# A block sum of the down projection on GpSimd, and the residual rows loaded at other units

## The chip, the cores and the metric

The kernel runs on one core of a Trainium2 chip. The core has a matrix engine (TensorE, in the profile PE, with its weight loads as PEld), a vector engine (VectorE, DVE), a scalar engine (ScalarE, ACT), GpSimd (POOL) and a queue that issues DMAs (SyncE, SP). Each runs its own instructions in order and waits for the others on semaphores. The metric is the device time of one execution in microseconds (us): the median of the runs.

## The reference

One encoder block on a sequence of 2048 positions with a model width of 1024, all in float32. An RMS norm, a projection, two groups of heads and an output projection come first; then

```
x = x + conv_ffn(rms_norm(x))      # up projection, causal convolution, SiLU gate, down projection
out = rms_norm(x)

conv_ffn: (silu(g) * val) @ w_down # (2048 x 2816) times (2816 x 1024)
```

The change lies in the last product, `@ w_down`, and in the sum with the residual `x` behind it.

## The kernel before

The kernel is one long program in stages: projection, attention and gating, output projection, up projection, and last the down projection, `down()`, which starts near 1985 us of the span. The sequence is worked in two halves of 1024 positions. Activations go through DRAM: the gated result of the up projection is in `act_d[half][f]` (22 blocks of 128 channels by 1024 positions), the residual rows of a half in `rows_d[half][i]` (8 tiles of 128 positions by 1024 columns, 512 KB each).

**Products.** For each half the down projection is a 2 x 2 block product made with seven products in place of eight (a scheme of Strassen's kind): positions are split into two blocks of 512, columns into two of 512, channels into two groups of 11 blocks. The products run in the order P1, P2, P7, P6, P5, P4, P3, each over the 11 block pairs j. One (half, product, j) is a **unit**; there are 2 x 7 x 11 = 154, counted from 0, so P2 of half 0 starts at unit 11, P7 at 22, P6 at 33, P5 at 44. A unit is 12 matmuls: four tiles t of 128 positions, each with three matmuls, because float32 is done with a high and a low part of each operand (high x high, high x low, low x high).

**Preparation.** `prep(u)` readies unit u. It loads the weights `wr` (512 columns; 256 KB) from `w_down` or from weight sums made earlier (`tw_d`), splits them with `both()` (ACT casts the high part `wh`, line 1017; DVE subtracts for the low part `wl`, line 1018), loads the activation blocks it needs (`x11`, `x12`, `x21`, `x22`, 256 KB each, kept for the rest of the half), forms the block sum that its product takes, and splits that into `xh` and `xl` in the same way. The sums are: P7 x11 - x21 into `xs` (line 1346); P6 x21 + x22 in place (line 1349) and from it minus x11 (line 1351); P5 takes x21 as it then is, and beside it x12 - x11 in place (line 1355) for P3. All these have both inputs in SBUF. `ready(u)` calls `prep` two units ahead of the matmuls; there are five buffers for each of the split parts, and four for `wr`.

**Banks.** There are eight accumulators in PSUM, in two banks of four (A and B). P1 starts in A and P2 in B; after P2, B is begun anew by P7. P6, P5 and P3 go on accumulating in A, P4 in B. After each product the four tiles are added to the residual rows (line 1479, the eviction: PSUM plus SBUF). The plan says to which rows and columns:

```
PLAN = dict(P1=("A", 0, 0, False), P2=("B", 0, 0, True), P7=("B", 1, 1, False), P6=("A", 1, 0, False),
            P5=("A", 1, 1, True), P4=("B", 1, 0, True), P3=("A", 0, 1, True))
```

The entries are the bank, the block of rows (0: row tiles 0 to 3, 1: row tiles 4 to 7), the column half, and whether that part is then complete. So P1 and P2 both add to rows 0 to 3, and P7 is the first to add to rows 4 to 7. Where the next product goes on in the same bank (P6 to P5), its first matmul waits for the eviction of that tile. P2, P6 and P3 end with a tail in which the last units are done tile by tile, so that evictions can start before the product has ended.

**Rows.** `row(half, i)` loads a row tile at its first call and afterwards returns what is there. It is called in the loop over units (which loads ahead) and in the eviction loop (`x = row(half, 4 * blk + t)`). Rows 0 to 3 and rows 4 to 7 have four buffers each. The load is tied behind the last weight load issued before it (`issue_after(self.w_ins)`).

**Order.** The order within each engine's queue and the semaphores are made by the framework: it goes through the program with a timeline of its own, takes what is ready by that timeline in the order of the program text, and fixes the result. On the chip the order of each queue no longer changes. An instruction later in the text may thus stand earlier in its queue: the subtractions of line 1355 for P5, for example, stand in DVE's queue from 2071 us on, while PE is in P7.

At the start of the down projection the last two blocks of the up projection are still finished on DVE (`up_conv`), their results stored by POOL's DMA queue, and the memory of their tiles is then given to the blocks `x12`, `x21`, `x22`. Beside that, POOL does in this stage only small sums of 128 x 1 for the final norm (lines 1402, 1421, 1422).

Of the kernel before, what the change touches and what calls it, by code (L numbers as in the profile page):

```python
# [12 lines left out]
ALU = mybir.AluOpType  # L13
# [67 lines left out]
class Block:  # L81
# [1221 lines left out]
    def down(self):  # L1303
        nc, tc = self.nc, self.tc
        tt = nc.vector.tensor_tensor
# [10 lines left out]
        def ring(tag, i, n, dt=F32):  # L1316

            return self.til(dp, [P, TB], dt, tag + "+" if i % n < 2 else tag)

        def block(half, j, name):  # L1320

            k = half, j, name
            if k not in raw:
                raw[k] = ring(name, j, NJ) if name == "x11" else self.til(pools[name], [P, TB], F32, name)
                f = j + (NJ if name[2] == "2" else 0)
                b = int(name[1]) - 1
                with tc.issue_after(self.w_ins):
                    self.dma(raw[k], self.act_d[half][f][:, b * TB:(b + 1) * TB])
            return raw[k]

        def prep(u):
            half, n, j = units[u]
            w = ring("wr", u, 4)
            src = dict(P1=w_down[:, j, 0:TB], P2=w_down[:, j + NJ, 0:TB], P3=w_down[:, j + NJ, TB:D],
                       P5=self.tw_d[j][:, 0, 0:TB], P7=self.tw_d[j][:, 0, TB:D], P4=self.tw_d[j][:, 1, 0:TB], P6=self.tw_d[j][:, 1, TB:D])[n]
            self.w_ins = self.dma(w, src).ins
            wp = [ring(tag, u, 5, F32R) for tag in ("wh", "wl")]
            self.both(wp, w)
            x = lambda name: block(half, j, name)
            if n == "P1":  # L1340
                v = x("x11")
            elif n == "P2":
                v = x("x12")
            elif n == "P7":
                v = xs.pop() if xs else self.til(dp, [P, TB], F32, "xs")
                tt(v, x("x11"), x("x21"), op=ALU.subtract)
            elif n == "P6":

                tt(x("x21"), x("x21"), x("x22"), op=ALU.add)
                v = x("x11")  # L1350
                tt(v, x("x21"), v, op=ALU.subtract)
            elif n == "P5":
                v = x("x21")

                tt(x("x12"), x("x12"), x("x11"), op=ALU.subtract)
            elif n == "P4":
                v = x("x22")
            else:
                v = x("x12")
            if u == 1:  # L1360

                late.append(dp.tile([P, D], F32, name="gf"))
                xs.append(self.til(dp, [P, TB], F32, "xs"))
            xp = [ring(tag, u, 5, F32R) for tag in ("xh", "xl")]
            self.both(xp, v)
            parts[u] = wp, xp

        def ready(u):
            while len(parts) <= min(u, len(units) - 1):
                prep(len(parts))  # L1370

        def mms(bank, u, t, fresh, last):
            w, x = parts[u]
            j = units[u][2]
            ts = slice(t * P, (t + 1) * P)
            kw = {} if fresh else {"skip_group_check": True}
            for i, k in ((0, 0), (0, 1), (1, 0)):
                nc.tensor.matmul(bank[t], lhsT=x[i][:, ts], rhs=w[k], start=fresh and j == 0 and i + k == 0,  # L1378
                                 stop=last and i == 1, **kw)

        def row(half, i):
            if (half, i) not in rows:
                x = rows[half, i] = self.til(dp if i < 4 else pools["x12"], [P, D], F32, "xo")
                with tc.issue_after(self.w_ins):
                    self.dma(x, self.rows_d[half][i])
            return rows[half, i]

        def square(half, i, col):
            x = row(half, i)
            if (half, i, "s") not in rows:  # L1390
                rows[half, i, "s"] = self.til(dp, [P, 2], F32, "s2")
            jk = jks.pop() if jks else self.til(dp, [P, TB], BF16, "jk")
            nc.scalar.activation(jk, x[:, col * TB:(col + 1) * TB], AF.Square,
                                 accum_out=rows[half, i, "s"][:, col:col + 1])

        def end_row(half, i):
            x, ss = rows[half, i], rows[half, i, "s"]
            rs = self.til(dp, [P, 1], F32, "rs")
            tt(rs, ss[:, 0:1], ss[:, 1:2], op=ALU.add)
            nc.vector.tensor_scalar(rs, rs, 1.0 / D, EPS, ALU.mult, ALU.add)  # L1400
            r = self.til(dp, [P, 1], F32, "rstd")
            nc.gpsimd.tensor_tensor(r, rs, self.mhalf[:, 0:1], op=ALU.pow)
            t0 = half * HALF + i * P
            for col in range(2):
                cs = slice(col * TB, (col + 1) * TB)
                nc.vector.scalar_tensor_tensor(x[:, cs], x[:, cs], r, gf[:, cs], op0=ALU.mult, op1=ALU.mult)
                self.dma(self.out[0, t0:t0 + P, cs], x[:, cs])

        def half_done(i):

            x = row(1, i)
            s = self.til(dp, [P, 1], F32, "rs")
            nc.vector.tensor_scalar(s, rows[1, i, "s"][:, 0:1], D * EPS, None, ALU.add)
            tt(x[:, 0:TB], x[:, 0:TB], gf[:, 0:TB], op=ALU.mult)
            rows[i] = s

        def last_row(i):

            x, ss, s = rows[1, i], rows[1, i, "s"], rows[i]
            r = self.til(dp, [P, 1], F32, "rstd")  # L1420
            nc.gpsimd.tensor_scalar(r, ss[:, 1:2], s, 1.0 / D, ALU.add, ALU.mult)
            nc.gpsimd.tensor_tensor(r, r, self.mhalf[:, 0:1], op=ALU.pow)
            t0 = HALF + i * P
            a, b = slice(0, TB), slice(TB, D)
            nc.vector.scalar_tensor_tensor(x[:, b], x[:, b], r, gf[:, b], op0=ALU.mult, op1=ALU.mult)
            self.dma(self.out[0, t0:t0 + P, b], x[:, b])
            nc.scalar.activation(x[:, a], x[:, a], AF.Copy, scale=r)
            self.dma(self.out[0, t0:t0 + P, a], x[:, a])
# [8 lines left out]
        def finish_up():  # L1437

            with tc.issue_after(low1):
                self.up_conv(NF - 1)  # L1440
            self.fps.close()
            d2 = es.enter_context(tc.tile_pool(name="downp2", side="right", **kw))
            for n in ("x12", "x21", "x22"):
                pools[n] = d2
            self.dma(gf, self.a["norm_final_g"].unsqueeze(0).broadcast_to([P, D]))
# [7 lines left out]
        for half in range(2):  # L1453
            for n in self.PRODUCTS:
                which, blk, col, whole = PLAN[n]
                fresh = n in ("P1", "P2", "P7")
                if fresh:
                    banks[which] = [self.til(pp, [P, TB], F32, "D") for _ in range(4)]
                bank = banks[which]
                tail = {"P2": 2, "P6": 2, "P3": 4 if half else 2}.get(n, 0)  # L1460
                cs = slice(col * TB, (col + 1) * TB)
                for j in range(NJ - tail):
                    if u == 2:
                        finish_up()
                    ready(u + (4 if (half, n) == (1, "P3") else 2))
                    for t in range(4):
                        mms(bank, u, t, fresh, j == NJ - 1)
                    u += 1
                    if (half, n) == (1, "P3") and j < 4:
                        half_done(j)  # L1470
                    if n in ("P1", "P2") and 4 <= j < 8:
                        row(half, j - 4 + (4 if n == "P2" else 0))
                for t in range(4):
                    if tail:
                        ready(u + tail + max(0, t - 1))
                    for m in range(tail):
                        mms(bank, u + m, t, fresh, m == tail - 1)
                    x = row(half, 4 * blk + t)
                    tt(x[:, cs], bank[t], x[:, cs], op=ALU.add)  # L1479
                    if whole:  # L1480
                        square(half, 4 * blk + t, col)
                        if (half, n) == (1, "P3"):
                            last_row(t)
                        elif n in ("P4", "P3"):
                            end_row(half, 4 * blk + t)
                u += tail
# [77 lines left out]
```

## Time and profile before

| | us |
|---|---|
| median of 3 runs | 2423.89 (2420.24 to 2425.25) |
| the profiled execution | 2419.3 |
| its span, first to last instruction | 2417.5 |

Of the page's parts, the busy times are by engine with the share of the span; the chain is the work that ended last, followed back from the end to what released each step; a group of instructions is line, engine, operation, output and inputs by name, shapes and count, then busy time, mean ns of one, and the idle time before them with what ended it. Three lines of the page and of one window give the setting:

```profile
PEclk9999999999999999999999999999999999999999
L1378 PE MATMUL D<-wh,xh 128*128 128x512 f32 x368 | 140.8, 389 | 1.2 <-DVE xo L1479 1.2
L994 POOL TENSOR_TENSOR tw<-tw 128x512 f32<-128x512 f32 x44 | 67.0, 1522 | 44.9 <-DMA tw<-in_w_down_dram 42.9
```

The first is the granted clock of TensorE in 40 slices of the span, at full speed throughout. The second is a group of the down projection's matmuls; one is shown as 389 ns long, but they are pipelined and start 0.23 us apart. The third is a group on POOL in an earlier stage: sums of weights of the same shape as the block sums above.

### The profile page before, as it was taken

What the parts mean: (1) busy time and instruction counts of PE and PEld (TensorE: products, weight loads), DVE (VectorE), ACT (ScalarE), POOL (GpSimd) and SP (SyncE); (2) the same over time, 40 slices, a digit from 0 to 9 for tenths busy, and PEclk for the clock granted to TensorE, in tenths of its full rate; (3) what the DMA queues carried; (4) which work ended last, traced back from release to release, by engine and by line L of the source; (5) the groups of instructions that cost most, each with busy time, mean ns of one, the idle gap of its engine ahead of it and who ended that gap; (6) DMA issues with size and microseconds to landing.
All of it is one profiled execution on the core that took longest, in us unless ns stands there. A gap on an engine that the chain in (4) does not pass through costs nothing.

```text
span 2417.5 us, 33292 instructions
## 1 busy us (share of the span) xinstructions
PE 2392.8 (99%) x11288; PEld 1998.3 (83%) x11288; DVE 1764.8 (73%) x3108; ACT 1355.3 (56%) x2652; POOL 323.2 (13%) x315
## 2 busy tenths in 40 slices
PE   9999999999999999999999999999999999999998
PEld 7888888988888888888888888888888888888887
DVE  6447776665568778878878774598888877857875
ACT  4246767644456555767677764365555455454444
POOL 4114140100241221211111101100000000000001
PEclk9999999999999999999999999999999999999999
DMA  8673635668855444555445555312222238438633
GB/s 278 182 241 111 206 100 175 186 192 265 260 191 183 160 163 161 165 173 185 146 151 182 170 195 203 116 53 96 79 86 81 87 96 310 157 99 300 205 118 122
DMA packets 246042, 400.58 MB, mean 166 GB/s; under 512 B 51224, under 2 KB 110744, under 8 KB 244448
## 3 DMA queue, kind: packets, MB, share of 16 engines
q1 hardware_dynamic: 240832, 374.34, 47.9%
q0 software_dynamic: 5040, 24.12, 2.5%
q8 instruction: 89, 1.46, 0.2%
q14 instruction: 81, 0.66, 0.1%
HBM read 304.79 MB, written 93.72 MB: 165 GB/s over the span
## 4 chain that ended last, share of the span: by engine, by line
PE 87%; DMA 2%; DVE 1%; ACT 1%; issue 0%; POOL 0%; POOLq 0%; SPq 0%; ACTq 0%; DVEq 0%
PE mm L211 37%; PE D L1378 16%; PE A L1176 3%; PE A L1178 3%; PE A L1177 3%; PE o L822 3%; PE o L821 3%; PE s L773 2%; PE s L772 2%; PE s L834 2%; PE s L833 2%; PE B L1178 2%; PE B L1177 2%; PE B L1176 2%; PE C L1176 1%; PE C L1177 1%
## 5 line engine op out<-in xcount | busy, mean ns | idle before, releaser
L211 PE MATMUL mm<-tlo,whi 128*128 128x512 f32 x896 | 351.4, 392 | 0.0
L211 PE MATMUL mm<-thi,wlo 128*128 128x512 f32 x896 | 351.1, 392 | 0.0
L211 PE MATMUL mm<-thi,whi 128*128 128x512 f32 x896 | 350.5, 391 | 0.5 <-DVE vn L519 0.5
L211 PE MATMUL mm<-whi,thi 128*128 128x512 f32 (+2 forms) x768 | 275.9, 360 | 6.1 <-DVE vn L519 4.4
L211 PE MATMUL mm<-wlo,thi 128*128 128x512 f32 (+2 forms) x768 | 275.5, 359 | 2.2 <-DVE wlo L164 2.2
L211 PE MATMUL mm<-whi,tlo 128*128 128x512 f32 (+2 forms) x768 | 274.8, 358 | 0.0
L150 POOL TENSOR_SCALAR whi<-raw 128x1024 fp32r<-128x1024 f32 (+3 forms) x114 | 132.4, 1163 | 963.2 <-PE mm L211 741.5
L781 ACT ACTIVATE s<-s,part 128x512 f32<-128x512 f32 (+3 forms) x261 | 154.7, 593 | 145.3 <-DVE part L776 80.6
L211 PEld LDWEIGHTS mm<-thi,whi 128*128 128x128 f32 x896 | 168.4, 188 | 35.2 <-issue 0.7
L211 PEld LDWEIGHTS mm<-thi,wlo 128*128 128x128 f32 x896 | 168.5, 188 | 34.1
L211 PEld LDWEIGHTS mm<-tlo,whi 128*128 128x128 f32 x896 | 168.5, 188 | 33.7
L845 DVE TENSOR_TENSOR pl<-e,ph 128x512 fp32r<-128x512 f32 (+1 forms) x218 | 142.9, 662 | 69.6 <-ACT ph L844 40.5
L211 PEld LDWEIGHTS mm<-whi,thi 128*128 128x128 f32 x768 | 145.9, 190 | 26.3 <-DVE vn L519 4.6
L164 DVE TENSOR_TENSOR wlo<-raw,whi 128x1024 fp32r<-128x1024 f32 (+2 forms) x106 | 135.1, 1276 | 44.0 <-POOL whi L150 43.0
L839 ACT ACTIVATE e<-s 128x512 f32<-128x512 f32 (+1 forms) x222 | 114.5, 530 | 91.8 <-DVE s L837 44.0
L211 PEld LDWEIGHTS mm<-wlo,thi 128*128 128x128 f32 x768 | 145.9, 190 | 22.7 <-DVE wlo L164 3.4
L211 PEld LDWEIGHTS mm<-whi,tlo 128*128 128x128 f32 x768 | 145.9, 190 | 19.3
L844 ACT ACTIVATE ph<-e 128x512 fp32r<-128x512 f32 (+1 forms) x218 | 120.6, 563 | 38.7 <-PE o L821 36.6
L1378 PE MATMUL D<-wh,xh 128*128 128x512 f32 x368 | 140.8, 389 | 1.2 <-DVE xo L1479 1.2
L1378 PE MATMUL D<-wl,xh 128*128 128x512 f32 x368 | 141.4, 389 | 0.0
L1378 PE MATMUL D<-wh,xl 128*128 128x512 f32 x368 | 137.5, 389 | 0.0
L776 DVE TENSOR_REDUCE part<-s 128x1 f32<-128x512 f32 x149 | 98.6, 684 | 20.9 <-PE s L773 19.9
(1858 smaller groups left out, 5850.4 us busy)
## 6 DMA issues: line engine op xcount, KB each, us to landing
raw<-in_w_up_dram SPq DMA_DIRECT2D x72, 512.0 KB
m<-kx SPq DMA_DIRECT2D x134, 256.0 KB
m<-kx SPq DMA_DIRECT2D x160, 136.0 KB
x<-act SPq DMA_DIRECT2D x84, 256.0 KB
v<-vd SPq DMA_DIRECT2D x67, 256.0 KB
raw<-in_w_in_dram SPq DMA_DIRECT2D x28, 512.0 KB
raw<-in_w_out_dram SPq DMA_DIRECT2D x24, 512.0 KB
tw<-in_w_down_dram SPq DMA_DIRECT2D x11, 1024.0 KB
```

The source lines that it names most:

```text
L150: self.cast_ins = self.nc.gpsimd.tensor_scalar(out, in_, 1.0, 0.0, ALU.mult, ALU.add).ins
L164: nc.vector.tensor_tensor(lo, raw, f32(hi), op=ALU.subtract)
L211: self.last_mm = self.nc.tensor.matmul(ps, lhsT=a[k], rhs=b[k], start=i == 0, stop=i == 3 * n - 1).ins
L776: nc.vector.tensor_reduce(dst, ps, axis=AX.X, op=ALU.min)
L781: nc.scalar.activation(ps[:, :n], ps[:, :n], AF.Exp, scale=-1.0, bias=dst, accum_out=ls[:, tt, sb:sb + 1])
L839: nc.scalar.activation(e[:, c], ps[:, c], AF.Exp, scale=-1.0)
L844: nc.scalar.activation(ph[:, c], e[:, c], AF.Copy)
L845: nc.vector.tensor_tensor(pl[:, c], e[:, c], f32(ph[:, c]), op=ALU.subtract)
L1176: mm(ps, lhsT=xh[:, ks], rhs=yh[:, k, :], start=fresh and k == 0, stop=False, **kw)
L1177: mm(ps, lhsT=xh[:, ks], rhs=yl[:, k, :], start=False, stop=False, **kw)
L1178: mm(ps, lhsT=xl[:, ks], rhs=yh[:, k, :], start=False, stop=k == 3, **kw)
L1378: nc.tensor.matmul(bank[t], lhsT=x[i][:, ts], rhs=w[k], start=fresh and j == 0 and i + k == 0, stop=last and i == 1, **kw)
```

## The change

Two edits in `down()`. In P6's preparation the first of the two block sums, x21 + x22, is issued on GpSimd in place of VectorE; the second, which needs it, stays on VectorE. In the loop over units the condition under which a row tile is loaded ahead is another: before, at units 4 to 7 of P1 (rows 0 to 3) and of P2 (rows 4 to 7); now, at units 0, 2, 4, 6 of P2 (rows 0 to 3) and units 1, 3, 5, 7 of P7 (rows 4 to 7). The eviction loop, with its own call of `row`, is as it was.

```
             elif n == "P6":

-                tt(x("x21"), x("x21"), x("x22"), op=ALU.add)
+                nc.gpsimd.tensor_tensor(x("x21"), x("x21"), x("x22"), op=ALU.add)
                 v = x("x11")
                 tt(v, x("x21"), v, op=ALU.subtract)
...
                     u += 1
                     if (half, n) == (1, "P3") and j < 4:
                         half_done(j)
-                    if n in ("P1", "P2") and 4 <= j < 8:
-                        row(half, j - 4 + (4 if n == "P2" else 0))
+                    if n in ("P2", "P7") and j < 8 and j % 2 == (n == "P7"):
+                        row(half, j // 2 + (4 if n == "P7" else 0))
                 for t in range(4):
```

More of the change, by code (lines that the diff above doesn't have):

```diff
@@ L1347, in prep @@
             elif n == "P6":
-                tt(x("x21"), x("x21"), x("x22"), op=ALU.add)
+                nc.gpsimd.tensor_tensor(x("x21"), x("x21"), x("x22"), op=ALU.add)
                 v = x("x11")
@@ L1470, in down @@
                         half_done(j)
-                    if n in ("P1", "P2") and 4 <= j < 8:
-                        row(half, j - 4 + (4 if n == "P2" else 0))
+                    if n in ("P2", "P7") and j < 8 and j % 2 == (n == "P7"):
+                        row(half, j // 2 + (4 if n == "P7" else 0))
                 for t in range(4):
```

## The prediction

> **What bounds the kernel now.** I read the page first, then who waits for TensorE, then the chain that ended last, each cut to the down projection (1985 us to the end), and last the DVE's own stretch there.
>
> ```profile
> span 2417.5 us, 33292 instructions
> PE 2392.8 (99%) x11288; PEld 1998.3 (83%) x11288; DVE 1764.8 (73%) x3108; ACT 1355.3 (56%) x2652; POOL 323.2 (13%) x315
> ```
>
> PE is busy for 99% of the span, so a change away from PE can win no more than the places where PE waits. In the down projection these are few. The waits of PE, longest first in total:
>
> ```profile
> PE D L1378 <- DVE xo L1479: 1.4, 2, 1.2
> PE D L1378 <- ACT xh+_4041_19352 L1017: 1.1, 1, 1.1
> ```
>
> The last column is the longest single wait: 1.2 and 0.2 us for an eviction, 1.1 us for a half of an operand. The chain says where and why:
>
> ```profile
> 2002.97 8.03 DMA wr<-in_w_down_dram
> ...
> 2013.82 0.33 SPq L100
> ...
> 2014.24 4.14 DMA x<-act
> ...
> 2018.40 0.64 ACT xh+_4041_19352 L1017
> ...
> 2019.08 89.19 PE D L1378 x392
> ...
> 2109.53 0.69 DVE xo L1479
> ...
> 2110.36 1.86 PE D L1378 x7
> ```
>
> The 1.1 us lie between P1 and P2 of half 0 (PE starts P2 at 2019.08): a weight load took 8.03 us, which held up SP's next issue and with it the first x12 block. The 1.2 us lie between P6 and P5 (2110.36): bank A is evicted and then accumulated further, and the first eviction came late from the DVE. The DVE was late because it is full there. Windows from the first block sum of P6 (L1349) to the first eviction, one for each half:
>
> ```profile
> 2067.28:2109.53 42.25, 41.89 (x185) 34.34 (x183) 41.69 (x70) 18.29 (x32) 0.00 (x0) 1.00 0.46 150
> 2277.39:2319.43 42.04, 42.04 (x187) 34.83 (x186) 41.70 (x69) 18.85 (x33) 0.00 (x0) 1.00 0.45 152
> ```
>
> The columns are the length, then PE, weight loads, DVE, ACT and POOL, granted clock, DMA share, GB/s. The DVE runs 70 and 69 instructions in 42 us, 0.60 us each, and POOL runs none. PE has no reserve left against it, as one unit shows (time, length, engine, line):
>
> ```profile
> 2101.70 0.68 DVE L1018 TENSOR_TENSOR xl+_4252_20153<-x,xh+_4251_20152 128x512 fp32r<-128x512 f32 x1
> 2102.64 1.09 PE L1378 MATMUL D<-wh+_4248_20144,xl+_4252_20153 128*128 128x512 f32 x4
> ```
>
> The low half of unit 41 is finished at 2101.70 + 0.68 = 2102.38, and PE takes it 0.26 us later. So in P6 every microsecond that the DVE gains or loses soon reaches PE: a gain up to 1.4 us in both halves, a loss in full.
>
> **The change, part 1: the block sum.** It takes L1349 from the DVE, 11 times in each half, and gives POOL the same 11 adds.
>
> ```profile
> L1349 DVE TENSOR_TENSOR x<-x,x 128x512 f32<-128x512 f32 x11 | 7.5, 685 | 1.9 <-DMA x<-act 1.9
> 2110.73 1.88 DVE L1479 TENSOR_TENSOR xo<-D,xo 128x512 f32<-128x512 f32 x3
> 2277.39 0.69 DVE L1349 TENSOR_TENSOR x<-x,x 128x512 f32<-128x512 f32 x1 [0.54 <-DMA x<-act]
> ```
>
> The first is a group of the first window: count, busy us and mean ns, then the idle time before it and what ended it. One lasts 0.68 us, but they overlap: three in 1.88 us are (1.88 - 0.68) / 2 = 0.60 us apart. The DVE thus saves 11 x 0.60 = 6.6 us in each half, and the waits for the x22 block before L1349 (1.9 us in half 0, 0.5 us in half 1) pass to POOL. The subtraction L1351 then waits for POOL. Behind it on the DVE stand the low halves (L1018) for PE and the evictions; ACT waits for L1351 too, to cast xh.
>
> POOL's add of this very form exists in the trace: L994, 128x512 f32, two inputs in SBUF.
>
> ```profile
> L994 POOL TENSOR_TENSOR tw<-tw x44: 1279/1618/2152, 713.8 to 1359.4; 128x512 f32<-128x512 f32 x44
> 1128.52 4.71 POOL L994 TENSOR_TENSOR tw<-tw 128x512 f32<-128x512 f32 x3 [9.09 <-DMA tw<-in_w_down_dram]
> 1128.89 3.17 DVE L845 TENSOR_TENSOR pl<-e,ph 128x512 fp32r<-128x512 f32 x2 [0.50 <-PE o L822]
> 1131.98 1.79 DVE L845 TENSOR_TENSOR pl+_2398_10534<-e,ph+_2397_10533 128x512 fp32r<-128x512 f32 x1
> 1355.77 5.34 POOL L994 TENSOR_TENSOR tw<-tw 128x512 f32<-128x512 f32 x3
> 1358.07 0.68 DVE L776 TENSOR_REDUCE part<-dn 128x1 f32<-128x512 f32 x1
> ```
>
> The first row gives shortest, median and longest: 1.28, 1.62, 2.15 us. One add per unit fits into POOL, since a unit of PE is 12 matmuls (89.19 / 392 = 0.2275 us each), 2.73 us. POOL is not the trouble. The two engines stand in each other's way: during three adds of POOL, three DVE subtractions of two SBUF tensors, of L1349's shape and so of 0.68 us alone, end at 1131.98 + 1.79 = 1133.77, so they took 4.88 us from 1128.89 instead of 3 x 0.60 + 0.08 = 1.88. That is 3.0 us for three adds, 1.0 each; the third alone is 1.79 - 0.68 = 1.11 us too long. A DVE instruction that reads PSUM (L776) kept its 0.68 us beside POOL. In P6 all DVE work but the evictions is of the kind that is held up, and the DVE has no pause in which POOL could hide. I take the 1.1 us of the third, the one with both engines in step; the bounds are 0 (POOL falls into pauses) and 1.28 (the whole add).
>
> Per half: 11 x (1.1 - 0.60) = +5.5 us of DVE time. Off go the waits that pass to POOL (1.9 and 0.5) and the adds that fall on evictions (in the windows 4 P7 evictions of 0.60, so 2.4 of 42 us, times 12.1 us: 0.7). Half 0: 5.5 - 1.9 - 0.7 = +2.9. Half 1: 5.5 - 0.5 - 0.7 = +4.3. Together **+7.2 us**, as PE waits in P6 or at its end. The credits are 1.9 + 0.5 + 2 x 0.7 = 3.8 us, so part 1 breaks even at a hold-up of 0.60 + 3.8 / 22 = 0.77 us an add.
>
> By the Trainium skill ("SBUF — State Buffer", section "Who interferes with whom"), a DVE instruction with two SBUF inputs and a GpSimd instruction that reads SBUF exclude each other for the whole instruction, and one with a single SBUF input goes free. The rows agree on who is held up, and show 1.0 to 1.1 us of the 1.28.
>
> **Part 2: the rows.** What the code does is not quite what the new condition says. After P1 the eviction loop calls row(half, 0..3) for column 0, so rows 0 to 3 are now loaded there, by that call, and the new calls at P2's units 0, 2, 4, 6 find them loaded. Only rows 4 to 7 really move, from P2's units 4 to 7 to P7's units 1, 3, 5, 7. No transfer is added; 16 remain.
>
> ```profile
> xo<-rows SPq DMA_DIRECT2D x8, 512.0 KB
> 1995.00 0.58 SPq L100 DMA_DIRECT2D xo<-rows  x1
> ...
> 2002.37 0.32 SPq L100 DMA_DIRECT2D xo<-rows  x1
> ...
> 2006.24 0.33 SPq L100 DMA_DIRECT2D wr+_4043_19368<-in_w_down_dram  x1
> ```
>
> Rows 0 to 3 of half 0 go out between 1995.00 and 2002.37, the last right ahead of the weights that took 8.03 us. In the new program they stand in one lump behind the weights of unit 12, the load of 2006.24, some 12 us before P1 ends (2018.0: PE's start at 2019.08 less its wait of 1.1).
>
> ```profile
> 2000.00:2010.00 10.00, 10.00 (x46) 8.28 (x45) 7.97 (x12) 4.95 (x9) 0.55 (x1) 1.00 1.04 411
> 2010.00:2020.00 10.00, 8.89 (x40) 7.05 (x39) 5.50 (x9) 5.36 (x9) 0.00 (x0) 1.00 0.80 265
> 2060.00:2070.00 10.00, 10.00 (x46) 8.27 (x45) 6.84 (x12) 3.50 (x7) 0.00 (x0) 1.00 0.55 177
> ```
>
> At 411 GB/s the lump of 4 x 0.524 MB lasts 5.1 us, so the rows are in by about 2012, before the evictions. Weights 8 to 11 no longer queue behind rows; the SP issue of 2013.82 and the x12 block come earlier by part of the 8.03 us. They have to come only 1.1 us earlier for the wait at 2019.08 to go: **-1.1 us**. The bounds are 0 and, for the lump lying ahead of x12, +5.1. Rows 4 to 7 leave P2 for P7, where the share is 0.55 and SP issues several units ahead; a row then lies up to 0.524 MB / 411 = 1.3 us ahead of a weight load, and the low halves of P7 are ready long before PE takes them:
>
> ```profile
> 2069.75 0.69 DVE L1018 TENSOR_TENSOR xl<-xs,xh 128x512 fp32r<-128x512 f32 x1
> ```
>
> This is P7's last unit; PE gets to it at 2019.08 + 21 x 2.73 = 2076.4, 6 us after. So I cost the move at nothing; without that cover it would be 1.3 us.
>
> **Sum:** +7.2 - 1.1 = +6.1 us. The profiled execution took 2419.3 us (span 2417.5 and 1.8 around it), so it would take 2425.4; the runs' median is 2423.89, 4.6 us above the profiled one, and the same +6.1 gives **2430.0 us**, 0.25% slower. A measurement of this kernel tells about 0.2% from no change (4.8 us).
>
> **The rivals.**
> 1. *The add is free* (not slower). Place: P6. POOL's adds fall into pauses of the DVE, so that the hold-up is near 0; it decides at 0.77 us, above which part 1 costs time. For it: with 6.6 us less work in each half the DVE could get pauses, and the scheduler may use them to put the low halves earlier. Against it: 41.7 of 42 us busy, and the stretched L845. Then all three waits go: -1.2 - 0.2 - 1.1 = -2.5, 2421.4 us. The Trainium skill ("Perfetto Trace Analysis", section "Optimizing Scalar/DVE Operations") says that moving work from a saturated DVE to GpSimd may pay, and in the same paragraph that between these two it might not; no run here shows it for P6.
> 2. *Half absorbed.* The hold-up is 1.0 us and a new order of the instructions puts the low halves ahead of P5's early subtractions (L1355, 11 in each window), which P6 doesn't need. At 1.0 us part 1 is 7.2 - 2 x 11 x 0.1 = +5.0; three of the L1355 put behind the first eviction take 3 x 0.60 = 1.8 us off each half: 5.0 - 3.6 - 1.1 = +0.3, 2424.2 us. Against it: the window of half 0 holds all 11 of them ahead of the eviction, and with a less loaded DVE they come earlier, not later.
> 3. *The whole add blocks.* The hold-up is 1.28 us, the shortest of L994's row, in place of 1.1: 2 x 11 x 0.18 = +4.0 on top, 2434.0 us. For it: single L845 rows may hide a part of the add in their own start. Against it: they show 1.0 to 1.1. This is the Trainium skill's rule of part 1 taken to the letter.
> 4. *The lump lies ahead of x12.* If SP issues the rows late, x12's first block comes up to 5.1 us later; with half of that, the 1.1 us stay and 2.6 come on top: 6.1 + 1.1 + 2.6 = +9.8, 2433.7 us. Against it: the load of 2006.24 stood 12 us ahead of P1's end.
>
> **How the numbers follow.** Forecast 0.47 (0.10 of it under 0.2%: at a hold-up of 1.0 it is 5.0 - 1.1 = +3.9); rival 1 0.18 (0.03 of it faster by over 0.2%); rival 2 0.15; rival 3 0.08; rival 4 0.12. Slower: 0.37 + 0.08 + 0.12 = 0.57. Same: 0.10 + 0.15 + 0.15 = 0.40. Faster: 0.03. The range runs from rival 1 (2421.5) to rivals 3 and 4 (2434): what lies outside is half of rival 1 and half of 3 and 4, 0.19.
>
> **What would show it.** In the new trace: DVE instructions of P6 (L1351, L1355, L1018) with single durations of 1.2 to 1.8 us where POOL's add runs, and evictions at 0.68; POOL's adds between 1.3 and 1.8 us; a PE wait of some 4 us in P6 or at 2110 and again near 2320; rows 0 to 3 issued together near 2006; no wait at 2019. The forecast is wrong if these DVE rows keep 0.68 us, if PE's waits in P6 shrink, or if the row lump makes P2 start later than now.

## The result, and the profile after

| | before | after |
|---|---|---|
| median of 8 runs, us | 2420.68 (2419.61 to 2425.25) | 2431.24 (2427.94 to 2435.83) |
| the profiled execution, us | 2419.3 | 2429.82 |

The ratio of after to before is 1.0040, 95% interval 1.0029 to 1.0051: slower by some 9.7 us (7.0 to 12.3). Ratios, here and below, leave out single runs far longer than the rest (2630 to 8937 us), which came in several kernels, the one before among them. The page of the kernel after:

```profile
span 2428.1 us, 33379 instructions
PE 2396.9 (99%) x11288; PEld 1996.7 (82%) x11288; DVE 1771.8 (73%) x3086; ACT 1353.9 (56%) x2652; POOL 359.4 (15%) x337
```

22 instructions went from DVE (3108 before) to POOL (315 before), yet DVE is busy 7.0 us longer than the 1764.8 us it had with more to do. The waits of PE in the down projection of the kernel after:

```profile
PE D L1378 <- DVE wl L1018: 4.4, 6, 1.5
PE D L1378 <- ACT xh+_4037_19344 L1017: 1.2, 1, 1.2
PE D L1378 <- DVE wl+_4243_20119 L1018: 0.5, 1, 0.5
PE D L1378 <- DVE wl+_4761_22202 L1018: 0.5, 1, 0.5
```

The wait for an eviction (xo, 1.4 us) has gone. PE now waits for low halves, many times, inside P6. The one wait for xh at P2's start is still there. Windows of the kernel before, and then of the kernel after, cut where PE starts a product: P1 with P2 of half 0, P6 of half 0, P6 of half 1 (columns as in the prediction: length, then PE, weight loads, DVE, ACT, POOL).

```profile
1987.10:2049.14 62.04, 60.64 (x266) 49.32 (x264) 44.77 (x66) 33.02 (x57) 0.55 (x1) 1.00 0.91 322
2079.06:2110.36 31.30, 30.11 (x134) 24.62 (x132) 31.30 (x53) 15.11 (x26) 0.00 (x0) 1.00 0.46 151
2289.99:2320.27 30.28, 30.09 (x133) 24.61 (x132) 29.98 (x51) 14.13 (x24) 0.00 (x0) 1.00 0.43 146
```

```profile
1989.23:2051.43 62.20, 60.66 (x265) 49.33 (x264) 43.99 (x66) 32.31 (x54) 0.54 (x1) 1.00 0.87 300
2081.35:2116.29 34.94, 31.46 (x133) 24.39 (x132) 33.75 (x48) 13.12 (x24) 12.96 (x7) 1.00 0.41 136
2295.81:2330.91 35.10, 31.79 (x133) 24.31 (x132) 35.10 (x47) 12.69 (x24) 10.56 (x7) 1.00 0.42 134
```

P6 is longer by 34.94 - 31.30 = 3.64 and 35.10 - 30.28 = 4.82 us: +8.46. P1 with P2 is longer by 0.16. P7 is the time from the end of the first window to the start of the second, 29.92 us in both kernels. The rest of the 10.6 us between the two spans lies ahead of the change: the stage is entered at 1989.23 in place of 1987.10, 2.1 us later, though the queues up to there are in the same order in both kernels. Experiment 5 takes that up.

Inside P6 the DVE of the kernel after looks like this (start, length, engine, line; in brackets the idle time ahead and what ended it):

```profile
2068.23 0.69 DVE L1346 TENSOR_TENSOR xs<-x,x 128x512 f32<-128x512 f32 x1 [2.51 <-DMA x<-act]
...
2071.91 1.76 DVE L1351 TENSOR_TENSOR x11+_4110_19622<-x,x11+_4110_19622 128x512 f32<-128x512 f32 x1 [1.18 <-POOL x L1349]
...
2085.92 1.78 DVE L1355 TENSOR_TENSOR x<-x,x 128x512 f32<-128x512 f32 x1
2087.62 0.68 DVE L1018 TENSOR_TENSOR xl+_4222_20023<-x,xh+_4221_20022 128x512 fp32r<-128x512 f32 x1
...
2090.63 1.28 DVE L1479 TENSOR_TENSOR xo<-D,xo 128x512 f32<-128x512 f32 x2
...
2094.84 0.68 DVE L1018 TENSOR_TENSOR wl<-wr,wh 128x512 fp32r<-128x512 f32 x1
2096.70 0.69 DVE L1351 TENSOR_TENSOR x<-x,x 128x512 f32<-128x512 f32 x1 [1.19 <-POOL x L1349]
...
2102.02 1.78 DVE L1018 TENSOR_TENSOR wl+_4243_20119<-wr+_4241_20116,wh+_4242_20118 128x512 fp32r<-128x512 f32 x1
2104.33 1.78 DVE L1351 TENSOR_TENSOR x<-x,x 128x512 f32<-128x512 f32 x1
```

And POOL beside it:

```profile
2085.64 1.51 POOL L1349 TENSOR_TENSOR x<-x,x 128x512 f32<-128x512 f32 x1 [2.00 <-DMA x<-act]
2090.32 1.54 POOL L1349 TENSOR_TENSOR x<-x,x 128x512 f32<-128x512 f32 x1 [3.17 <-DMA x<-act]
2093.22 3.45 POOL L1349 TENSOR_TENSOR x<-x,x 128x512 f32<-128x512 f32 x1 [1.35 <-DVE wl L1018]
...
2101.47 1.79 POOL L1349 TENSOR_TENSOR x<-x,x 128x512 f32<-128x512 f32 x1 [2.33 <-DMA x<-act]
2104.07 1.49 POOL L1349 TENSOR_TENSOR x<-x,x 128x512 f32<-128x512 f32 x1 [0.81 <-DMA x<-act]
```

Lay one over the other. The add of 2085.64 meets L1355 at 2085.92: 1.78 us in place of 0.68, 1.10 too long. Those of 2101.47 and 2104.07 do the same to wl and to L1351. The add of 2090.32 runs beside two evictions, which read PSUM: 1.28 us for two, as before, nothing lost. And the add of 2093.22 was itself held up: it takes 3.45 us while DVE passes through work of 0.68 us each, and then DVE, which needs its result, stands for 1.19 us. So an add costs the DVE about as much either way: 1.1 us as a hold-up, or 1.2 us as a wait for POOL.

### The profile page after: what moved, and what is told of

The parts are those of the page before. It is cut to its first block, busy times and chain, and to the rows that moved or that the text cites. A ratio compares the mean times of both kernels' runs of the same rounds, so it can differ in the third digit from the quotient of the medians.

```text
span 2428.1 us, 33379 instructions
## 1 busy us (share of the span) xinstructions
PE 2396.9 (99%) x11288; PEld 1996.7 (82%) x11288; DVE 1771.8 (73%) x3086; ACT 1353.9 (56%) x2652; POOL 359.4 (15%) x337
## 4 chain that ended last, share of the span: by engine, by line
PE 85%; DVE 2%; DMA 2%; ACT 1%; issue 1%; POOL 0%; SPq 0%; POOLq 0%; ACTq 0%; DVEq 0%
PE mm L211 37%; PE D L1378 15%; PE A L1176 3%; PE A L1178 3%; PE A L1177 3%; PE o L822 2%; PE o L821 2%; PE s L773 2%; PE s L772 2%; PE s L834 2%; PE s L833 2%; PE B L1177 2%; PE B L1178 2%; PE B L1176 2%; PE C L1176 1%; PE C L1177 1%
```

## The experiments

The kernels are named by what they do. Ratios are to the kernel before, run on the same chip beside them, with the 95% interval. "P6" is always the time from the start of PE in P6 to its start in P5, half 0 and half 1, from one profiled execution each.

### 1. Which of the two edits costs the time

**The block sum alone** (rows as before):

```
-                tt(x("x21"), x("x21"), x("x22"), op=ALU.add)
+                nc.gpsimd.tensor_tensor(x("x21"), x("x21"), x("x22"), op=ALU.add)
```

> Part 1 alone: x21 + x22 of P6 on GpSimd, the rows loaded as before. The hold-up theory: the add costs the DVE 1.1 us each where it saved 0.6, so the two P6 products get longer by what the changed kernel showed (31.3 to 34.9 us and 30.3 to 35.1 us), P1 of half 0 stays at 32.0 us, and the total is about 8.4 us above the kernel before. If the moved rows had a share in the loss, P6 would be clearly shorter than 34.9 and 35.1 us here.

Measured: 2431.27 us, ratio 1.0036 (1.0023 to 1.0048); P6 36.05 and 35.55 us.

**The rows alone** (the new condition, sum on VectorE):

```
-                    if n in ("P1", "P2") and 4 <= j < 8:
-                        row(half, j - 4 + (4 if n == "P2" else 0))
+                    if n in ("P2", "P7") and j < 8 and j % 2 == (n == "P7"):
+                        row(half, j // 2 + (4 if n == "P7" else 0))
```

> Part 2 alone: the add stays on the DVE. If the rows 0 to 3 in one lump take the place of the rows in between as what the first blocks of P2 queue behind, P1 of half 0 keeps its 32.1 us and the total is the kernel before within 1 us; the prediction's term would make it 30.9 us and the total 1.1 us less. P6 stays at 31.3 and 30.3 us in both cases; a share of the rows in the loss would show as a longer P6 or P7 (now 29.9 us).

Measured: 2420.94 us, ratio 0.9998 (0.9988 to 1.0008); P6 30.44 and 30.28 us. The whole loss is that of the block sum. The rows give nothing and take nothing that can be measured.

### 2. A hold-up, or a wait for POOL's result?

The sum on POOL could cost time because DVE waits for it (a dependency), or because POOL's instruction holds DVE up whatever it computes. To separate them, P6 keeps its sum on VectorE and POOL makes an added sum of the same form that nobody reads:

```
                 tt(x("x21"), x("x21"), x("x22"), op=ALU.add)
+                nc.gpsimd.tensor_tensor(spare[0], x("x22"), late[0][:, 0:TB], op=ALU.add)
```

> The kernel before with one more add on GpSimd in each unit of P6, x22 plus the norm's gains into a tile that nobody reads; the DVE keeps its own add. The hold-up theory: each of these adds holds the DVE for 1.1 us although nothing waits for its result, 11 x 1.1 = 12.1 us in each half less 0.7 for those beside evictions, so P6 gets longer by about 11.4 us in each half (to 42 us) and the total by about 22 us. The rival, that the loss comes from L1351 waiting for GpSimd's result: no change, P6 at 31.3 and 30.3 us.

Measured: 2445.15 us, ratio 1.0091 (1.0075 to 1.0106); P6 41.48 and 43.58 us, so 10.2 and 13.3 longer, 23.5 together or 23.5 / 22 = 1.07 us for each add. Nothing waits for these sums. The windows of the two P6 (the third column from the right is the granted clock), then POOL and DVE of that kernel at one of the sums:

```profile
2081.26:2122.74 41.48, 33.46 (x133) 25.28 (x132) 41.48 (x58) 15.03 (x27) 10.56 (x8) 0.96 0.39 125
2302.36:2345.94 43.58, 34.10 (x133) 25.78 (x132) 42.20 (x57) 14.74 (x26) 10.88 (x8) 0.92 0.38 123
```

```profile
2086.70 1.63 POOL L1350 TENSOR_TENSOR spare<-x,gf 128x512 f32<-128x512 f32 x1 [0.68 <-DMA x<-act]
```

```profile
2086.50 0.68 DVE L1349 TENSOR_TENSOR x<-x,x 128x512 f32<-128x512 f32 x1
2087.10 1.78 DVE L1356 TENSOR_TENSOR x<-x,x 128x512 f32<-128x512 f32 x1
2088.80 0.68 DVE L1018 TENSOR_TENSOR xl+_4222_20028<-x,xh+_4221_20027 128x512 fp32r<-128x512 f32 x1
```

The same 1.78 us as in the changed kernel. So a hold-up alone, with no result waited for, costs over 1 us an add. A part of the 10.2 and 13.3 us may be another thing, the clock, which was below 1.00 in both halves; the last section has it. Free of that are the stretched DVE rows themselves: 22 of them, 11.4 and 11.8 us over their 0.68 us in the two halves, 1.05 us for each add.

### 3. What on POOL holds the DVE up

Two more added instructions that nobody needs. First one that reads only one tensor:

```
+                nc.gpsimd.tensor_scalar(spare[0], x("x22"), 1.0, 0.0, ALU.mult, ALU.add)
```

> The kernel before with one copy on GpSimd in each unit of P6, of the x22 block into a tile that nobody reads: one input in SBUF instead of two, about 0.64 us alone (the 128x528 copies of L150). If any read of SBUF by GpSimd holds a two-input DVE instruction, each holds it for some 0.64 - 0.18 = 0.46 us, 5 us in each half: P6 at 36 and 35 us, the total up by about 9. If only GpSimd's two-input adds hold the DVE, P6 stays at 31.3 and 30.3 us.

Measured: 2425.54 us, ratio 1.0011 (1.0002 to 1.0020); P6 32.22 and 33.06 us. I had expected some 5 us in each half; 0.9 and 2.8 came. A row of POOL, then one of DVE early in P6's preparation:

```profile
2088.90 25.12 POOL L1350 TENSOR_SCALAR spare<-x 128x512 f32<-128x512 f32 x4 [2.18 <-DMA x<-act]
```

```profile
2073.49 1.10 DVE L1349 TENSOR_TENSOR x<-x,x 128x512 f32<-128x512 f32 x1
```

Where POOL's copy gets in, the DVE instruction beside it takes 1.10 us, 0.42 too long; there are 5 such rows in half 0 and 6 in half 1. But in each half one copy does not get in for long: of the 25.12 us of the four copies in POOL's row the first takes 22.51, and the DVE's instructions keep 0.68 to 0.69 us all the while. Here it was POOL that was held up, until the DVE evicted P6's first tile (2110.84), which reads PSUM. So fewer DVE instructions were stretched than there are copies, and each by less.

Then one that only writes, with a read of 128x1 ahead of it that ties it to the same moment:

```
+                nc.gpsimd.tensor_scalar(spare[0][:, 0:1], x("x22")[:, 0:1], 1.0, 0.0, ALU.mult, ALU.add)
+                nc.gpsimd.memset(spare[0], 0.0)
```

> The kernel before with, in each unit of P6, a copy of one column (128x1) of x22 on GpSimd, to set the pace, and then a fill of 128x512 that only writes SBUF (0.53 us). If the hold-up comes of GpSimd's reads, only the small copy counts (0.2 to 0.3 us, at most 0.1 us of hold-up each): P6 within 1 us of 31.3 and 30.3 us. If writes hold the DVE as well, 0.35 us and more each: P6 longer by 4 us in each half.

Measured: 2421.30 us, ratio 0.9995 (0.9985 to 1.0004); P6 31.41 and 30.52 us, 0.1 and 0.2 longer. A group of POOL in that kernel's window of both P6, and two rows of its timeline, POOL's and DVE's:

```profile
L1351 POOL MEMSET spare<- 128x512 f32 x22 | 11.6, 527 | 1.3
```

```profile
2086.70 22.29 POOL L1350 TENSOR_SCALAR spare<-x 128x1 f32<-128x1 f32 x1 [1.69 <-DMA x<-act]
```

```profile
2108.84 0.70 DVE L1482 TENSOR_TENSOR xo<-D,xo 128x512 f32<-128x512 f32 x1
```

The tiny read ahead of one of the fills stood for 22.29 us, again until that eviction. Of the 22 fills of a whole tile, 14 therefore ran beside the busy DVE, whose rows there keep 0.68 to 0.69 us, and 8 only behind such a read, beside the evictions: they cost the DVE nothing. Of what was tried here, the two engines thus contend for reading, not for writing.

### 4. Is it the full DVE that turns a hold-up into time?

If so, the same sum on POOL must cost far less where the DVE has room. The 11 subtractions of line 1355 (needed by P3 only, which comes after P5 and P4) stand in the midst of P6's work. Tied behind the low half issued last before them, they leave the stretch in which PE is waiting. First with the block sum on POOL:

```
+                nc.gpsimd.tensor_tensor(x("x21"), x("x21"), x("x22"), op=ALU.add)
...
+                with tc.issue_after(self.low_ins):
+                    tt(x("x12"), x("x12"), x("x11"), op=ALU.subtract)
```

> Part 1 with P5's early subtraction (L1355) tied behind the low half of its own unit's weights, so that it no longer stands among P6's instructions on the DVE. The hold-up theory with a full DVE: the DVE has 11 x 0.6 = 6.6 us less to do in each P6, more than the 3.6 and 4.8 us lost, so P6 comes down to 30 to 31 us in both halves and the total to within 1.5 us of the kernel before. If P6's loss were the length of the chain through GpSimd (add, subtraction, cast, low half) and not a full DVE, P6 would stay near 35 us.

Measured: 2424.09 us, ratio 1.0005 (0.9996 to 1.0014); P6 31.97 and 31.02 us, a little over the 30 to 31 expected. Then the second edit alone, the sum on VectorE as before:

> The add stays on the DVE and the rows as before; only P5's early subtraction (L1355) is tied behind the low half of its own unit's weights, out of P6. The DVE then has 6.6 us less to do in P6 with no hold-up to pay: both P6 at 29.9 to 30.1 us, the eviction waits of 1.2 and 0.2 us gone, the total 1.4 us less, which is under what the runs can tell. If the eviction wait had another cause than a full DVE, P6 stays at 31.3.

Measured: 2419.70 us, ratio 0.9991 (0.9982 to 1.0000); P6 29.92 and 29.92 us. In half 0 the 11 subtractions now stand on the DVE from 2104.63 to 2129.12 us, not from 2071 us on. The windows of P6 in the two kernels, first with the sum on POOL, then on VectorE:

```profile
2082.37:2114.34 31.97, 30.43 (x134) 24.54 (x132) 27.68 (x39) 13.05 (x25) 10.55 (x7) 1.00 0.42 139
2293.96:2324.98 31.02, 30.38 (x133) 24.54 (x132) 27.48 (x40) 13.20 (x25) 10.29 (x7) 1.00 0.47 155
```

```profile
2081.03:2110.95 29.92, 29.92 (x134) 24.78 (x132) 28.73 (x49) 12.03 (x22) 0.00 (x0) 1.00 0.47 158
2290.47:2320.39 29.92, 29.92 (x134) 24.78 (x132) 27.61 (x47) 12.14 (x22) 0.00 (x0) 1.00 0.46 153
```

With room on the DVE the sum on POOL costs (31.97 - 29.92) + (31.02 - 29.92) = 3.15 us of P6, against 8.46 with a full one. It still costs: in that trace L1351 waits for POOL's sum ten times, 14.8 us in all. And the wait that the change was set against goes by the order of the queue alone: 29.92 us is 132 matmuls at 0.2267 us, PE without a pause.

### 5. What of the difference is chance, and what do the rows do?

Four profiled executions more, of one run each: before, after and the rows alone, unchanged, and a kernel in which the rows really come late. In that one the evictions of P1 are done in P2's units 5 to 8, so that the eviction loop no longer asks for rows 0 to 3 at P1's end:

```
+                    if n in ("P2", "P7") and j < 8 and j % 2 == (n == "P7"):
+                        row(half, j // 2 + (4 if n == "P7" else 0))
+                    if n == "P2" and 5 <= j < 9:
+                        t = j - 5
+                        x = row(half, t)
+                        tt(x[:, 0:TB], banks["A"][t], x[:, 0:TB], op=ALU.add)
...
+                    if n == "P1":
+                        continue
```

> The kernel before, unchanged, profiled once more. It says how far the lengths of the products differ between two executions of one kernel. If they are the kernel's own: down projection P1 31.98, P6 31.30 and 30.28 us again, to 0.1 us, and only the time at which the stage is entered (1987.10) moves. If the start-up of the stage varies: P1 differs by up to 0.6 us, and the 0.2 to 0.5 us that the row edit showed there prove nothing.

> The changed kernel, unchanged, profiled once more. If the lengthening of P6 is the change's: 34.9 and 35.1 us again to about 0.5 us (the block sum alone showed 36.05 and 35.55), so 8 to 9 us over the kernel before. P1: 32.1 again if the wait at P2's start is fixed by the order of the queues; else anywhere from 31.5 to 32.6.

> The row edit alone, profiled once more. Half 0's P6 was 30.44 us with it and 31.30 before. If the edit does that by another order on the DVE: 30.4 again. If it was chance: about 31.3. P1 31.5 again if the edit saves 0.5 us at P2's start, else up to 32.

> The kernel before with rows 0 to 3 really loaded at P2's units 0, 2, 4, 6: the evictions of P1 are moved into P2's units 5 to 8, so that the eviction loop no longer asks for the rows at P1's end. If the rows beside the weights are what makes PE wait at P2's start: P1 falls from 31.98 to 30.7 us or less, as in the version with both edits, P6 stays at 31.3 and 30.3 (a little less with the row edit's 0.9), in all 1 to 2 us less than before. If the wait there comes from the entry of the stage (x12's memory and the stores of the up projection): P1 stays at 31.5 to 32.

| | time, us | stage entered | P1 with P2, half 0 | P6, half 0 and 1 |
|---|---|---|---|---|
| before | 2419.30 | 1987.10 | 62.04 | 31.30, 30.28 |
| before, again | 2421.36 | 1988.66 | 62.31 | 31.12, 30.52 |
| after | 2429.82 | 1989.23 | 62.20 | 34.94, 35.10 |
| after, again | 2425.83 | 1985.45 | 63.00 | 34.68, 34.37 |
| rows alone | 2417.40 | 1986.59 | 61.59 | 30.44, 30.28 |
| rows alone, again | 2424.46 | 1988.74 | 64.57 | 31.62, 31.00 |
| rows really late | 2418.31 | 1986.87 | 60.62 | 30.51, 31.35 |

Three things follow. The time at which the stage is entered moves by up to 3.8 us from one execution of a kernel to the next, so two spans alone do not measure a change of this size. P6 moves less, by up to 0.7 us in a half of the kernels before and after: after less before is 8.46 us in the first pair and 69.05 - 61.64 = 7.41 us in the second, 7.9 in the mean. And the 30.44 us of P6 with the rows alone, which looked like a gain of 0.9 us, did not come again (31.62): it was chance, and there one half's P6 moved by 1.2 us.

The rows as the change has them make P1 with P2 vary from 61.59 to 64.57 us; before it was 62.04 and 62.31. With the rows really late it is 60.62, and the wait at P2's start is gone. In the kernel after, the row loads stand in one lump. SP's queue there, and three links of the chain of waits:

```profile
2008.06 0.33 SPq L100 DMA_DIRECT2D wr+_4039_19360<-in_w_down_dram  x1
2008.44 2.73 SPq L100 DMA_DIRECT2D xo<-rows  x4
2011.27 0.53 SPq L100 DMA_DIRECT2D wr+_4053_19400<-in_w_down_dram  x1
2011.90 0.56 SPq L100 DMA_DIRECT2D wr<-in_w_down_dram  x1
```

```profile
2011.90 8.05 DMA wr<-in_w_down_dram
...
2020.06 0.63 ACT wh L1017
2020.69 0.63 ACT xh+_4037_19344 L1017
2021.36 71.07 PE D L1378 x312
```

The rows no longer hold up weights 8 to 11, but now they hold up the load of 2011.90, two behind the lump: it takes 8.05 us, as its like did before (8.03). ACT's queue is in fixed order, with that wh right ahead of the xh with which P2 begins, so PE starts at 2021.36 after a wait of 1.2 us. The wait has the same size and another cause.

### 6. Both repairs together

Experiment 4's order of line 1355 with the late rows of experiment 5, all sums on VectorE:

> L1355 held as above, the add on the DVE, and P1's evictions put off to units 5 to 8 of P2, so that rows 0 to 3 really are loaded at P2's units 0, 2, 4, 6 and rows 4 to 7 at P7's 1, 3, 5, 7. No lump of rows then stands ahead of P2's first blocks: P1 of half 0 at 30.9 us instead of 32.0, P6 at 30.0, the total 2.5 us under the kernel before. If the wait at P2's start is not the rows' doing, P1 stays at 31.5 to 32.5 us.

Measured: 2418.40 us, ratio 0.9986 (0.9977 to 0.9995), a little faster than before; P6 29.92 and 29.92, P1 with P2 61.49 us. PE's waits in that kernel:

```profile
PE D L1379 <- DVE xo L1486: 0.7, 1, 0.7
PE D L1379 <- ACT xh+_3970_19084 L1017: 0.3, 1, 0.3
```

The 0.7 us is new: bank A's evictions, now inside P2, come late on the DVE behind a sum (line 1346) that waits for its block, so not all of the 1.4 us that the late rows won alone are kept.

## Why the prediction was right, and where it was not

The time forecast was 2430.0 us, and 2431.24 came; slower was the likeliest sign, and it is slower by more than 0.2%. But the forecast stood on a median of 2423.89 for the kernel before, which over 8 runs is 2420.68. The step itself was put at +6.1 us, and the interval of the ratio says 7.0 to 12.3. By the traces it is 7.9 in P6 and (0.16 + 0.69) / 2 = 0.4 at P2's start, 8.3 together. So the mechanism held, and its size was taken too small. That the two times lie 1.2 us apart is in part luck: the median that the forecast started from was 3.2 us high, and the step 2 us and more too low.

- **The bound: a full DVE in P6, where each microsecond lost reaches PE.** Right, and shown from both sides: 6.6 us of line 1355 taken out of the way bring P6 to 29.92 us, an idle add put in holds it up by 1.05.
- **The hold-up, 1.1 us.** Right: single rows of 1.76 to 1.79 us where 0.68 stood, for L1351, L1355 and L1018 alike, and 0.68 for evictions. Rival 3 (1.28, the whole add) falls with it, and so does rival 1 (nothing).
- **How many adds cost it.** Mis-sized. I took off 0.7 us in each half for adds that fall on evictions. In half 1 of the kernel after all 11 adds met an SBUF instruction (ten rows stretched by 1.1 us, one by 0.85: 11.8 us). That less 6.6 saved and 0.5 of x22's wait is +4.7, and +4.82 was measured. So near a match is luck in part: the DVE's waits for blocks in half 1 did not fall by 0.5 but rose from 0.87 + 0.54 = 1.41 to 1.17 + 0.66 = 1.83 us, with which the count is 11.8 - 6.6 + 0.4 = +5.6. In half 0, 8 rows were stretched (8.8 us) and the DVE waited twice for POOL (1.18 and 1.19): 11.2 us.
- **The credit of 1.9 us in half 0** for waits for x22 that pass to POOL. This step failed. In the prediction's count a wait that passes to POOL was gone; but POOL's sum is needed at once by L1351, and the DVE waits for it in turn. The rows above at 2071.91 and 2096.70 show it (they are in the 11.2 us), and the second profile of the kernel after has it again (1.21 and 1.17 us), as has the block sum alone, with six such waits. And the DVE got only some of the credit: 11.2 - 6.6 - 1.9 would be +2.7, and +3.64 came. It stood longer for a block of P7 instead, at line 1346: 2.51 us in the row above at 2068.23, against 1.77 us in the kernel before:

```profile
2064.61 0.69 DVE L1346 TENSOR_TENSOR xs<-x,x 128x512 f32<-128x512 f32 x1 [1.77 <-DMA x<-act]
```

Its waits for blocks from 10 us into P7 on were 1.77 + 1.38 + 0.55 = 3.70 us before and 0.50 + 2.51 = 3.01 us after (3.51 and 2.92 us in the second profiles). That is 0.7 less, not 1.9, and 11.2 - 6.6 - 0.7 is +3.9.

- **The rows, -1.1 us.** This step failed: +0.2 and +0.7 us in two pairs. The first part was as said: by the call in the eviction loop, rows 0 to 3 go out in one lump, behind the weights of unit 12, ahead of the evictions. The error was to ask only which load is set free, and not which stands behind the lump (experiment 5: 8.05 us). It was rival 4 in small, with a weight load in x12's place. That the lump's place is what matters is shown by the rows really late (60.62 us).
- **Rows 4 to 7, at no cost.** Right: P7 lasts 29.92 us before and after.
- **Rival 2, half absorbed by the order.** The order was not so: the scheduler kept line 1355 in P6's midst. But its price was real. With line 1355 behind, the changed sum costs 1.0005 of the time before in place of 1.0036.

Open stays why the block sum alone has a P6 some 1.6 to 2.6 us longer than the whole change has in two profiles (71.60 us in its only one, against 70.04 and 69.05); by the medians the two are alike. Its DVE waits for POOL six times, 8.7 us in all, where each profile of the whole change has two such waits, 2.4 us; why the order came out so, the runs do not show.

## What to carry to other kernels

In this kernel a full engine was not relieved by a helper whose reads hold it up: before moving an instruction, compare the time that it saves there (0.60 us) with the time that its twin elsewhere takes from the same engine (1.1 us), and add the wait for the result that comes back. Look first for work in the full stretch that nobody needs yet, and move it in the order of the queue, which here cost no engine anything. A load that is taken out of one queue position stands in front of something else at the next one; ask what is second and third behind it, and see whether a lazy call elsewhere in the program undoes the new place.

## What the hardware showed that I had not expected

**A read of POOL can be kept out for over 20 us.** POOL's sums of two SBUF tensors got in behind one DVE instruction or two (1.28 to 2.23 us each), but for one that got in only when the DVE stood still (the 3.45 us above). Of its reads with one input, one in each half was kept out far longer: 22.51 and 21.44 us (copies of 128x512), 22.29 and 20.97 us (128x1); the others ended within 3 us. These four ended while the DVE evicted P6's first tile. The Trainium skill ("SBUF — State Buffer", section "Who interferes with whom") says of the pair of ports that these engines share that whichever issues first has it for its whole instruction and the other blocks, and that a GpSimd instruction which only writes is not in the way of a DVE instruction with two SBUF inputs. The stretched rows and the fills agree. Why one read is let in after one instruction and another is kept out for tens of them, the runs do not show.

**A PE wait of two microseconds can cost twice.** In the second profile of the rows alone, PE waited 2.07 us at P2's start. Windows of 2 us from there (the third column from the right is the granted clock):

```profile
2018.00:2020.00 2.00, 1.60 (x8) 0.98 (x6) 0.29 (x1) 0.34 (x1) 0.00 (x0) 1.00 1.05 390
2020.00:2022.00 2.00, 0.33 (x1) 0.33 (x2) 1.68 (x3) 1.80 (x4) 0.00 (x0) 0.93 1.05 403
2022.00:2024.00 2.00, 2.00 (x6) 1.52 (x6) 2.00 (x5) 1.83 (x4) 0.00 (x0) 0.50 0.98 315
2024.00:2026.00 2.00, 2.00 (x8) 1.62 (x7) 2.00 (x5) 0.99 (x2) 0.00 (x0) 0.72 0.96 358
```

The clock falls to 0.50 and comes back some 3 us later; that is the 1.5 us by which its P2 is longer (31.64 against 30.09 us in the first profile). In the second profile of the kernel after PE waited 1.96 us at the same place, and the clock kept 1.00. With the idle add the clock kept 1.00 behind waits of 2.66 us (P2's start) and 2.44 us (P6 of half 0). It fell to 0.50 behind the next wait there, of 1.92 us, for some 3 us, and again in a wait of 5.28 us in P6 of half 1, for some 7 us. So waits of up to 1.7 us were paid once in all traces of the down projection, and from about 2 us on a second price can come, in some executions.

Which waits pay it need not be chance. In the clock records of a trace the stretches at 0.50 start whole multiples of 3.41 us apart: with the idle add at 2104.80, 2326.66 and, at the end of the kernel, 2439.30 us, 65 and 33 times 3.41 us. Cut into intervals by this beat, the waits of 1.92 and 2.07 us, which the lower clock followed, lie whole in one interval each, and those of 1.96, 2.44 and 2.66 us, which it did not follow, are split in two, with 1.81 us as the largest part. No run was made to test this.
